# RWKV time mixing: mixing every unit on VectorE instead of projecting two of them unmixed, and a reordered tail

## The chip, the cores and the metric

The kernel runs on one core of a Trainium2 chip. A core has five engines with a queue each: TensorE (matmuls), VectorE (elementwise, called DVE in the profile), ScalarE (ACT, activations and copies with a scale), GpSimd (POOL) and SyncE (SP, which only issues transfers here). The metric is the device time of one execution in microseconds (us), as the median over several runs.

## The reference

```python
x_prev = np.zeros_like(x)
x_prev[:, 1:, :] = x[:, :-1, :]
xv = x * time_mix_v + x_prev * (1 - time_mix_v)
xr = x * time_mix_r + x_prev * (1 - time_mix_r)
v = xv @ value_weight
r = xr @ receptance_weight
out = (1 / (1 + np.exp(-r)) * v) @ output_weight
```

x is 16 x 2048 x 256 in fp32 and every weight is 256 x 256. The key projection of the full reference does not reach the output. So each row needs two mixed inputs, two projections, a sigmoid, a product z and an output projection.

## The kernel before

The 16 x 2048 rows are cut into 64 units of 512 rows (a batch has 4). A unit passes through these steps:

- The rows arrive in SBUF (x_unit and x_bf). TensorE transposes them, eight 128 x 128 blocks (`transposes`, L189), so that the 256 features lie on partitions in two halves, ko = 0 and 1. ScalarE copies the result into xt (L199 for fp32, L206 for bf16). Rows are laid out so that four "slots" of 128 columns hold rows j, j+1, j+2, j+3 of each partition's run. The row before a row is then the same column of the slot before, and only one extra slot per unit has to be filled by small copies (`wrap_slots`, L393 and L394).
- The mix. The weights are multiplied by time_mix once, so the mixed input is x + c * x_prev with c = 1/time_mix - 1. VectorE makes the product c * x_prev (`scale`, L239) and then adds x (`add`, L263), for the receptance (m = 0) and the value (m = 1). From some unit on the product of ko = 1 is made by GpSimd (`scale_pool`, L250); near the end ScalarE makes some (`scale_act`, L471).
- TensorE projects the mixed input (`project`, L274: four matmuls of 512 columns) to r and to v, R and V below. ScalarE applies the sigmoid to r (L492). VectorE multiplies it with v, which gives z (L521).
- TensorE multiplies z with the output weight (`out_matmuls`, L298, called O below), ScalarE copies the result to SBUF (L331), and SP issues the store. O of a unit follows one unit later.

Units 0 and 1 differ. The receptance of unit 0 and the value of unit 1 are not mixed: `project_unmixed` (L288) multiplies x_prev with a second weight w_prev = (1 - time_mix) * w and x with w_bf, eight matmuls instead of four. VectorE prepares w_prev at L412 and L429, from tm_prev (L167).

The order of the work on each engine is the order in which the program issues it (`manual_schedule`); an instruction waits at the head of its queue until what it reads is ready. The main loop over g writes that order out. Dictionaries say in which pass what is made for later units: `products[g]` (products on VectorE), `sums[g]` (adds ahead of z of unit g), `held[g]` (adds behind it), `pooled[g]` (products for GpSimd). `advance(limit)` issues transposes up to a unit, T1, T2 and so on below. Each of the PSUM pools ps_v, ps_r and ps_o has one buffer, and ps_t has two.

At the end `last_unit` takes unit 63 in two halves of 256 columns. It projects r by halves, then for each half: value projection, z (L359), and one half of O of unit 62. Then follows O of unit 63: slots 0 and 1 together in ps_v, copied by VectorE, slot 2 copied by ScalarE, slot 3 copied by VectorE (copies at L315, stores at L308). Slot 2 is stored from the ScalarE queue, the others from SP.

At the start small matmuls on zeros (`warm_up`, L140) keep TensorE at work while the first transfers are under way: 21, then 2, and 15 after the first transposes.

Of the kernel before, what the change touches and what calls it, by code (L numbers as in the profile page):

```python
# [15 lines left out]
def kernel(  # L16
# [110 lines left out]
    w_prev = consts.tile([P, 2, KO, D], BF16)  # L127
# [26 lines left out]
    tm_prev = consts.tile([P, 2, KO], FP32)  # L154

    def coefficients():
        ps = ps_o_pool.tile([P, 2, KO], FP32, name="psum_o")
        nc.tensor.transpose(
            out=ps.rearrange("p m k -> p (m k)"), in_=tm_rows, identity=ident_f[: 2 * KO, : 2 * KO]
        )  # L160
        tm = consts.tile([P, 2, KO], FP32)
        nc.vector.tensor_copy(out=tm, in_=ps)
        nc.vector.tensor_scalar(
            out=tms, in0=tm, scalar1=0.0, scalar2=1e-30, op0=ALU.is_equal, op1=ALU.mult
        )
        nc.vector.tensor_tensor(out=tms, in0=tms, in1=tm, op=ALU.add)
        nc.vector.tensor_scalar(  # L167
            out=tm_prev, in0=tm, scalar1=-1.0, scalar2=1.0, op0=ALU.mult, op1=ALU.add
        )
        nc.vector.reciprocal(c_sb, tms)  # L170
        nc.vector.tensor_scalar(out=c_sb, in0=c_sb, scalar1=-1.0, scalar2=None, op0=ALU.add)
# [110 lines left out]
    def project_unmixed(ps, g, m, mo):  # L282

        c = g * (UJ + 1) * P
        parts = [(w_prev[:, m, ko], ko, c) for ko in range(KO)]
        parts += [(w_bf[:, m, ko], ko, c + P) for ko in range(KO)]
        for n, (w, ko, lo) in enumerate(parts):
            nc.tensor.matmul(  # L288
                out=ps[:, mo, :],
                lhsT=w[:, mo * P : (mo + 1) * P],  # L290
                rhs=xt[0][:, ko, lo : lo + TU],
                start=(n == 0),
                stop=(n == len(parts) - 1),
            )

# [47 lines left out]
    def last_unit(g):  # L343
# [13 lines left out]
        for h, (lo, hi) in enumerate(cols):  # L357
            project(banks[2 + h], g, 1, lo, hi)
            nc.vector.tensor_tensor(  # L359
                out=z_sb[:, :, lo:hi], in0=s_sb[:, :, lo:hi], in1=banks[2 + h], op=ALU.mult  # L360
            )
# [46 lines left out]

    first_transposes()
    tile_for(0)  # L410
    for ko in range(KO):
        nc.vector.tensor_scalar(  # L412
            out=w_prev[:, 0, ko, :],
            in0=w_f32[:, 0, ko, :],
            scalar1=tm_prev[:, 0, ko : ko + 1],
            scalar2=None,
            op0=ALU.mult,
        )
    nc.vector.tensor_scalar(
        out=w_bf[:, 0, 0, :], in0=w_f32[:, 0, 0, :], scalar1=tms[:, 0, 0:1], scalar2=None, op0=ALU.mult  # L420
    )
    nc.scalar.activation(
        out=w_bf[:, 0, 1, :], in_=w_f32[:, 0, 1, :], func=ACT.Copy, scale=tms[:, 0, 1:2]
    )
    scale(pieces(0)[1])
    add(pieces(0)[1])
    for w, scale_by in [(w_bf, tms), (w_prev, tm_prev)]:
        for ko in range(KO):
            nc.vector.tensor_scalar(  # L429
                out=w[:, 1, ko, :],  # L430
                in0=w_f32[:, 1, ko, :],
                scalar1=scale_by[:, 1, ko : ko + 1],
                scalar2=None,
                op0=ALU.mult,
            )
# [11 lines left out]
    for u in range(2, NU):  # L447
# [31 lines left out]
    for g in range(NU - 1):  # L479
        ps_r = ps_r_pool.tile([P, KO, TU], FP32, name="psum_r")  # L480
        if g == 0:
            project_unmixed(ps_r, 0, 0, 0)
            advance(1)
            project_unmixed(ps_r, 0, 0, 1)
            for ko in range(KO):
                wrap_slots(pieces(1)[0], ko)
                scale(pieces(1)[0], (ko,))
            last = add(pieces(1)[0])
        else:
            project(ps_r, g, 0)  # L490
        s_sb = zpool.tile([P, KO, TU], BF16, name="s_sb")
        nc.scalar.activation(out=s_sb, in_=ps_r, func=ACT.Sigmoid)  # L492
        advance(START_T[g] if g < len(START_T) else g + LOOK)
        for p in products.get(g + 1, []):
# [15 lines left out]
        pool, name = (ps_o_pool, "psum_o") if g == 1 else (ps_v_pool, "psum_v")  # L510
        ps_v = pool.tile([P, KO, TU], FP32, name=name)
# [50 lines left out]
```

## Time and profile before

| | |
|---|---|
| median of 4 runs | 213.64 us (213.39 to 214.43) |
| profiled execution, its time | 213.33 us |
| its span (first to last instruction event) | 211.6 us |
| TensorE busy | 202.4 us, 96% |
| VectorE busy | 193.0 us, 91% |
| ScalarE busy | 185.8 us, 88% |
| GpSimd busy | 76.5 us, 36% |
| granted TensorE clock, mean | 0.994 |

In the rows of a timeline the first number is the start in us from the beginning of the span and the second the time that the group takes. Then come the engine, the line of the kernel, the operation, what it writes and reads, the sizes, and how many instructions were merged (x4). In brackets stands how long the engine had been idle before and what ended that. PEld is TensorE's loading of weights, which overlaps with matmuls. Consecutive instructions of an engine overlap a little in the records, so the distance between two starts is shorter than the duration shown. In the chain of work that ended last each row is a start, a time and the engine and line that held the chain then.

### The profile page before, as it was taken

To read this page: it belongs to the slowest core of one execution; us is meant where nothing else is said; L and a number is where in the kernel's file an instruction comes from. 1 tells how busy PE (TensorE), PEld (TensorE's weight loads), DVE (VectorE), ACT (ScalarE), POOL (GpSimd) and SP (SyncE) were. 2 spreads that over 40 slices of the span, in tenths; PEclk is the share of its full clock that TensorE was granted. 3 is DMA by queue.
4 is the path that set the end of the run, shared out by engine and by line. 5 is a ranking of instruction groups with operands and counts; after the bars stand their busy time and mean duration, and the time that the engine had idled before them with its cause. 6 is when DMAs were issued, how large, how long until landed. Compare 5 with 4: busy or idle time off the path is not lost.

```text
span 211.6 us, 4191 instructions
## 1 busy us (share of the span) xinstructions
PE 202.4 (96%) x1565; PEld 135.1 (64%) x1593; DVE 193.0 (91%) x321; ACT 185.8 (88%) x203; POOL 76.5 (36%) x106
## 2 busy tenths in 40 slices
PE   8789999999999999999999999999999999999991
PEld 7456665666666666666666666666666666665570
DVE  2789999999999999999999999999999999999971
ACT  3559999998999999999999999999999999999881
POOL 2701231334354435434452444335344432444200
PEclk9999999999999999999999999999999999999997
DMA  5999999999989998999989999897999944433475
GB/s 163 300 213 221 239 249 259 297 205 360 218 217 263 296 228 325 197 345 181 285 243 232 336 192 349 156 318 208 274 299 206 367 204 198 198 149 152 198 299 200
DMA packets 10140, 52.04 MB, mean 246 GB/s; under 512 B 1028, under 2 KB 2056, under 8 KB 5000
## 3 DMA queue, kind: packets, MB, share of 16 engines
q0 software_dynamic: 3008, 16.12, 44.1%
q1 hardware_dynamic: 6960, 35.52, 41.5%
q8 instruction: 12, 0.20, 0.3%
q10 hardware_dynamic: 152, 0.13, 0.2%
q14 instruction: 8, 0.07, 0.1%
HBM read 34.34 MB, written 33.55 MB: 321 GB/s over the span
## 4 chain that ended last, share of the span: by engine, by line
PE 74%; DVE 11%; DMA 5%; issue 4%; ACT 3%; POOL 1%; DVEq 0%; SPq 0%; POOLq 0%
PE psum_o L298 22%; PE psum_v L274 20%; PE psum_r L274 20%; PE ps_t L189 10%; DMA x_unit<-in_x_dram 5%; DVE mix L263 4%; DVE z_sb L521 3%; DVE mix L239 3%; ACT s_sb L492 2%; ACT xt_first L206 1%; PE psum_o L288 1%; ACT o_sb L331 0%; PE ps_t L274 0%; POOL mix L250 0%; DVE o_sb L315 0%
## 5 line engine op out<-in xcount | busy, mean ns | idle before, releaser
L250 POOL TENSOR_SCALAR mix<-xt,c_sb 128x1024 bf16<-128x1024 bf16 (+1 forms) x55 | 60.3, 1096 | 101.9 <-DVE mix L263 94.6
L263 DVE TENSOR_TENSOR mix<-mix,xt 128x1024 bf16<-128x1024 bf16 x112 | 78.1, 699 | 2.9 <-DVE mix L239 0.5
L521 DVE TENSOR_TENSOR z_sb<-s_sb,psum_v 128x1024 bf16<-128x1024 bf16 x62 | 75.5, 1217 | 4.6 <-PE psum_v L274 2.0
L331 ACT COPY o_sb<-psum_o 128x1024 f32<-128x1024 f32 x60 | 61.0, 1017 | 11.9 <-PE psum_o L298 11.9
L274 PEld LDWEIGHTS <-w_bf 128*128 128x128 bf16 x512 | 47.6, 98 | 33.7 <-issue 1.5
L492 ACT ACTIVATE s_sb<-psum_r 128x1024 bf16<-128x1024 f32 x63 | 65.1, 1033 | 0.5 <-PE psum_r L288 0.2
L274 PE MATMUL psum_v<-mix,w_bf 128*128 128x512 bf16 (+1 forms) x242 | 63.2, 377 | 0.8 <-DVE z_sb L521 0.2
L298 PE MATMUL psum_o<-wo_bf,z_sb 128*128 128x256 bf16 x488 | 63.4, 273 | 0.2
L274 PE MATMUL psum_r<-mix,w_bf 128*128 128x512 bf16 (+1 forms) x235 | 62.4, 377 | 0.6
L298 PEld LDWEIGHTS <-z_sb 128*128 128x128 bf16 x512 | 50.0, 98 | 19.0 <-DVE z_sb L359 0.3
L206 ACT COPY xt<-ps_t 128x1024 bf16<-128x1024 bf16 x56 | 57.0, 1022 | 0.0
L189 PEld LDWEIGHTS <-x_bf 128*128 128x128 bf16 x488 | 32.1, 98 | 13.5
L189 PE MATMUL ps_t<-ident,x_bf 128*128 128x128 bf16 x488 | 36.7, 219 | 0.3
L239 DVE TENSOR_SCALAR mix<-xt,c_sb 128x1024 bf16<-128x1024 bf16 (+1 forms) x63 | 27.7, 451 | 0.0
L263 DVE TENSOR_TENSOR mix<-mix,xt_first 128x1024 bf16<-128x1024 bf16 x14 | 9.5, 685 | 0.1
L106 POOL DMA_DIRECT2D x_bf<-in_x_dram x14 | 8.1, 576 | 0.0
L239 DVE TENSOR_SCALAR mix<-xt_first,c_sb 128x512 bf16<-128x512 bf16 x24 | 7.1, 348 | 0.3
L250 POOL TENSOR_SCALAR mix<-xt_first,c_sb 128x512 bf16<-128x512 bf16 x4 | 2.8, 692 | 12.6 <-DVE xt_first L394 12.6
L206 ACT COPY xt_first<-ps_t 128x1024 bf16<-128x1024 bf16 x5 | 5.2, 1037 | 1.1 <-PE ps_t L189 1.1
L140 PE MATMUL ps_t<-zeros 128*128 128x128 bf16 x38 | 3.8, 275 | 1.0 <-DVE zeros L84 1.0
L199 ACT CAST xt_first<-ps_t 128x512 bf16<-128x512 f32 x4 | 2.1, 589 | 2.7 <-PE ps_t L189 2.7
L140 PEld LDWEIGHTS <-zeros 128*128 128x128 bf16 x38 | 3.2, 125 | 1.0 <-DVE zeros L84 1.0
(67 smaller groups left out, 48.9 us busy)
## 6 DMA issues: line engine op xcount, KB each, us to landing
out_dram<-o_sb SPq DMA_DIRECT2D x30, 1024.0 KB, 8.3
x_bf<-in_x_dram POOLq DMA_DIRECT2D x14, 1024.0 KB, 11.4
x_bf<-in_x_dram POOLq DMA_DIRECT2D x5, 256.0 KB, 8.2
out_dram<-o_sb SPq DMA_DIRECT2D x5, 256.0 KB, 2.7
x_unit<-in_x_dram SPq DMA_DIRECT2D x2, 512.0 KB, 6.3
x_unit<-in_x_dram SPq DMA_DIRECT2D x2, 256.0 KB, 2.9
out_dram<-o_sb SPq DMA_DIRECT2D x1, 512.0 KB, 2.7
w_f<-n_receptance_weight_dram SPq DMA_DIRECT2D x1, 256.0 KB, 4.9
```

The costliest lines, as they stand in the source:

```text
L106: nc.gpsimd.dma_start(out=x_bf[b], in_=rows(b))
L140: nc.tensor.matmul(out=ps, lhsT=zeros, rhs=zeros, start=True, stop=True)
L189: nc.tensor.transpose(out=ps[:, jj * P : (jj + 1) * P], in_=src[:, jj, ko * P : (ko + 1) * P], identity=idn,)
L206: nc.scalar.copy(out=xt[b][:, :, c0 : c0 + TU], in_=ps)
L239: nc.vector.tensor_scalar(out=mix[b][:, m, ko, lo:hi], in0=xt[b][:, ko, c : c + hi - lo], scalar1=c_sb[:, m, ko : ko + 1], scalar2=None, o ...
L250: op = nc.gpsimd.tensor_scalar(out=mix[b][:, m, 1, lo:hi], in0=xt[b][:, 1, c : c + hi - lo], scalar1=c_sb[:, m, 1:2], scalar2=1.0, op0=ALU ...
L263: return nc.vector.tensor_tensor(out=mix[b][:, m, :, lo:hi], in0=mix[b][:, m, :, lo:hi], in1=xt[b][:, :, c : c + hi - lo], op=ALU.add,)
L274: nc.tensor.matmul(out=ps[:, mo, :], lhsT=w_bf[:, m, ko, mo * P : (mo + 1) * P], rhs=mix[b][:, m, ko, e * TU + lo : e * TU + hi], start=(k ...
L298: nc.tensor.matmul(out=ps[:, slot, :], lhsT=z[:, ko, jj * P : (jj + 1) * P], rhs=wo_bf[:, ko, :], start=(ko == 0), stop=(ko == KO - 1),)
L331: nc.scalar.copy(out=o_sb[b][:, j0 : j0 + UJ, :], in_=ps)
L492: nc.scalar.activation(out=s_sb, in_=ps_r, func=ACT.Sigmoid)
L521: nc.vector.tensor_tensor(out=z_sb, in0=s_sb, in1=ps_v, op=ALU.mult)
```

## The change

- `project_unmixed`, w_prev and tm_prev are removed. Unit 0's receptance is mixed as all others, in two pieces: slot 3 first, then slots 0 to 2. Both receptance weights are now made by VectorE (before, one of them by ScalarE). Of the value weights one is made by VectorE and one by ScalarE.
- In pass 0 the transposes T1 are issued ahead of R0. Behind R0 the loop now makes both mixes of unit 1, ahead of z of unit 0. Of unit 1's value mix the product of ko = 0 is made by ScalarE, issued ahead of unit 0's sigmoid.
- In pass 1 V1 and T3 are issued ahead of the mixes (these are on other engines), and unit 2's two mixes are made one after the other, product, add, product, add, both ahead of z of unit 1. The value add of unit 2 was behind that z before.
- The rule by which GpSimd makes the ko = 1 product of a value mix holds from unit 3 on (w > 1) instead of unit 4, and unit 3's slot copy is now made ahead of z of unit 1.
- In `last_unit` each half of O of unit 62 is issued ahead of the value projection of that half instead of behind it. O of unit 63 is taken in four single slots: slot 0 in ps_v copied by ScalarE, slot 1 in ps_o copied by VectorE, and slots 2 and 3 as before.

```diff
@@ last_unit
-        for h, (lo, hi) in enumerate(cols):
+        def value(h):
+            lo, hi = cols[h]
             project(banks[2 + h], g, 1, lo, hi)
             nc.vector.tensor_tensor(
                 out=z_sb[:, :, lo:hi], in0=s_sb[:, :, lo:hi], in1=banks[2 + h], op=ALU.mult
             )
+
+        def before(h):
             pool, name = [(ps_o_pool, "psum_o"), (ps_r_pool, "psum_r")][h]
             out_part(pool, name, z_prev, b, e - 1, h * H, H, by_act, nc.sync)
-        out_part(ps_v_pool, "psum_v", z_sb, b, e, 0, H, by_dve, nc.sync)
-        out_part(ps_t_pool, "ps_t", z_sb, b, e, H, 1, by_act, nc.scalar)
-        out_part(ps_t_pool, "ps_t", z_sb, b, e, H + 1, 1, by_dve, nc.sync)
+
+        before(0)
+        value(0)
+        before(1)
+        value(1)
+        out_part(ps_v_pool, "psum_v", z_sb, b, e, 0, 1, by_act, nc.sync)
+        out_part(ps_o_pool, "psum_o", z_sb, b, e, 1, 1, by_dve, nc.sync)
+        out_part(ps_t_pool, "ps_t", z_sb, b, e, 2, 1, by_act, nc.scalar)
+        out_part(ps_t_pool, "ps_t", z_sb, b, e, 3, 1, by_dve, nc.sync)
@@ head
+    def weight(m, ko, by_act=False):
+        ...
     first_transposes()
     tile_for(0)
     for ko in range(KO):
-        nc.vector.tensor_scalar(out=w_prev[:, 0, ko, :], ...)
-    nc.vector.tensor_scalar(out=w_bf[:, 0, 0, :], ...)
-    nc.scalar.activation(out=w_bf[:, 0, 1, :], ...)
+        weight(0, ko)
+    for lo, hi in [(UJ - 1, UJ), (0, UJ - 1)]:
+        part = (0, 0, lo * P, hi * P)
+        scale(part)
+        add(part)
     scale(pieces(0)[1])
     add(pieces(0)[1])
-    for w, scale_by in [(w_bf, tms), (w_prev, tm_prev)]:
-        ...
+    weight(1, 0)
     warm_up(WARM2)
@@ plan
-        (held if u - 1 < AHEAD else sums)[u - 1].append(p1)
+        (held if 2 <= u - 1 < AHEAD else sums)[u - 1].append(p1)
...
-            if paired or m == 1 and w > 2 and u != PAIRS - 1:
+            if paired or m == 1 and w > 1 and u != PAIRS - 1:
@@ main loop
     for g in range(NU - 1):
+        if g == 0:
+            advance(1)
+            weight(1, 1, by_act=True)
         ps_r = ps_r_pool.tile([P, KO, TU], FP32, name="psum_r")
+        project(ps_r, g, 0)
         if g == 0:
-            project_unmixed(ps_r, 0, 0, 0)
-            advance(1)
-            project_unmixed(ps_r, 0, 0, 1)
+            p0, p1 = pieces(1)
             for ko in range(KO):
-                wrap_slots(pieces(1)[0], ko)
-                scale(pieces(1)[0], (ko,))
-            last = add(pieces(1)[0])
-        else:
-            project(ps_r, g, 0)
+                wrap_slots(p0, ko)
+                scale(p0, (ko,))
+            add(p0)
+            scale_act(p1, (0,))
+            scale(p1, (1,))
+            last = add(p1)
         s_sb = zpool.tile([P, KO, TU], BF16, name="s_sb")
         nc.scalar.activation(out=s_sb, in_=ps_r, func=ACT.Sigmoid)
...
+        if g == 1:
+            ps_v = values()
...
+        left = list(sums[g])
         for p, kos in products[g]:
             if not (g - 1 + LOOK >= NU and p[1] == 1):
                 scale(p, kos)
-        for p in sums[g]:
+            if g == 1:
+                last = add(p)
+                left.remove(p)
+        for p in left:
             last = add(p)
...
-        if g == 1:
-            for mo in range(KO):
-                project_unmixed(ps_v, 1, 1, mo)
-            advance(3)
-        else:
-            project(ps_v, g, 1)
-        if g == 0:
-            advance(2)
+        if g != 1:
+            ps_v = values()
```

`values()` takes the PSUM buffer of V, issues `project(ps_v, g, 1)` and, for g < 2, `advance(g + 2)`.

More of the change, by code (lines that the diff above doesn't have):

```diff
@@ L126 @@
     w_bf = consts.tile([P, 2, KO, D], BF16)
-    w_prev = consts.tile([P, 2, KO, D], BF16)
     wo_bf = consts.tile([P, KO, D], BF16)
@@ L153 @@
     c_sb = consts.tile([P, 2, KO], FP32)
-    tm_prev = consts.tile([P, 2, KO], FP32)
     def coefficients():
@@ L166, in coefficients @@
         nc.vector.tensor_tensor(out=tms, in0=tms, in1=tm, op=ALU.add)
-        nc.vector.tensor_scalar(
-            out=tm_prev, in0=tm, scalar1=-1.0, scalar2=1.0, op0=ALU.mult, op1=ALU.add
-        )
         nc.vector.reciprocal(c_sb, tms)
@@ L280, in project @@
                 )
[L282 to L294, printed above, removed]
     def out_matmuls(ps, z, jj, slot):
@@ L407, in advance @@
             tnext += 1
+    def weight(m, ko, by_act=False):
+        scale_by = tms[:, m, ko : ko + 1]
+        if by_act:
+            nc.scalar.activation(
+                out=w_bf[:, m, ko, :], in_=w_f32[:, m, ko, :], func=ACT.Copy, scale=scale_by
+            )
+        else:
+            nc.vector.tensor_scalar(
+                out=w_bf[:, m, ko, :],
+                in0=w_f32[:, m, ko, :],
+                scalar1=scale_by,
+                scalar2=None,
+                op0=ALU.mult,
+            )
     first_transposes()
@@ L411 @@
     for ko in range(KO):
[L412 to L424, printed above, removed]
+        weight(0, ko)
[3 more added lines that the diff above has]
+        add(part)
     scale(pieces(0)[1])
     add(pieces(0)[1])
-    for w, scale_by in [(w_bf, tms), (w_prev, tm_prev)]:
[L428 to L435, printed above, removed]
+    weight(1, 0)
     warm_up(WARM2)
@@ L493, with values @@
         advance(START_T[g] if g < len(START_T) else g + LOOK)
+        def values():
+            pool, name = (ps_o_pool, "psum_o") if g == 1 else (ps_v_pool, "psum_v")
+            ps_v = pool.tile([P, KO, TU], FP32, name=name)
+            project(ps_v, g, 1)
+            if g < 2:
+                advance(g + 2)
+            return ps_v
+        if g == 1:
+            ps_v = values()
         for p in products.get(g + 1, []):
@@ L509 @@
             wrap_slots(p)
-        pool, name = (ps_o_pool, "psum_o") if g == 1 else (ps_v_pool, "psum_v")
-        ps_v = pool.tile([P, KO, TU], FP32, name=name)
-        if g == 1:
-            for mo in range(KO):
-                project_unmixed(ps_v, 1, 1, mo)
-            advance(3)
-        else:
-            project(ps_v, g, 1)
-        if g == 0:
-            advance(2)
+        if g != 1:
+            ps_v = values()
         z_sb = zpool.tile([P, KO, TU], BF16, name="z_sb")
```

## The prediction

> **What bounds the kernel now.** I read the busy row first. TensorE is busy 96% of the span, VectorE 91%, ScalarE 88%, so two or three engines are close to being the bound and an average does not decide. I therefore looked at the chain of work that ended last, in order of time, to see where it changes engine.
>
> ```profile
> 45.05 0.60 DVE mix L239 x3
> 46.04 0.47 issue
> 46.50 1.21 DVE z_sb L521
> 47.76 1.02 PE psum_v L274 x4
> 48.78 0.88 PE psum_o L298 x8
> 49.66 0.65 PE psum_r L274 x3
> ```
>
> Up to 46.50 the chain runs through VectorE (earlier pieces of the view, from 19.46 on, are the same lines L263, L239, L521 and L394). From 47.76 on it runs through TensorE. In the timeline value projections then start every 3.04 us (50.80, 53.85, 56.90), TensorE without a gap. The first 46 us are a VectorE chain of back-to-back work, and whatever moves that chain moves the rest of the kernel by the same amount. Over the stretch 19.5 to 46.5 VectorE is busy 27.00 of 27.00 us, TensorE 26.50.
>
> So the question is when VectorE can start the product z of unit 2, from where its cycle is unbroken. Its timeline at the head:
>
> ```profile
> 6.59 0.62 DVE L412 TENSOR_SCALAR w_prev<-w_f,tm_prev 128x256 bf16<-128x256 f32 x2 [1.64 <-DMA w_f<-n_receptance_weight_dram]
> 7.38 0.61 DVE L239 TENSOR_SCALAR mix<-xt_first,c_sb 128x512 bf16<-128x512 bf16 x2
> 8.02 0.69 DVE L263 TENSOR_TENSOR mix<-mix,xt_first 128x1024 bf16<-128x1024 bf16 x1
> ...
> 11.53 1.21 DVE L521 TENSOR_TENSOR z_sb<-s_sb,psum_v 128x1024 bf16<-128x1024 bf16 x1
> 13.29 0.23 DVE L394 COPY xt_first<-xt_first 128x254 bf16<-128x254 bf16 x1 [0.55 <-ACT xt_first L199]
> 13.63 1.14 DVE L239 TENSOR_SCALAR mix<-xt_first,c_sb 128x512 bf16<-128x512 bf16 x4
> 14.69 0.68 DVE L263 TENSOR_TENSOR mix<-mix,xt_first 128x1024 bf16<-128x1024 bf16 x1
> 15.29 1.22 DVE L521 TENSOR_TENSOR z_sb<-s_sb,psum_o 128x1024 bf16<-128x1024 bf16 x1
> ...
> 17.35 1.14 DVE L239 TENSOR_SCALAR mix<-xt_first,c_sb 128x512 bf16<-128x512 bf16 x4
> 19.46 1.22 DVE L521 TENSOR_TENSOR z_sb<-s_sb,psum_v 128x1024 bf16<-128x1024 bf16 x1 [0.23 <-ACT s_sb L492]
> ```
>
> Two things are to be seen. VectorE has only two waits after 6.59: 0.55 us before 13.29 (for the transposes of unit 2, whose transfer lands at 11.39) and 0.23 us before 19.46. Those are all the cover that added work can use. And starts are closer than durations: products of 512 columns follow each other every 0.26 us (0.35 long), adds every 0.60 (0.69 long), z every 1.13 (1.22 long). A product whose result the next add reads at once costs more, 0.64 us for two (7.38 to 8.02) where four independent ones cost 1.06 (13.63 to 14.69). I count starts.
>
> **TensorE, what is removed.** The unmixed projections take 8 matmuls where a mixed one takes 4, so 8 go: 4 in unit 0, 4 in unit 1, at 0.215 us each (8 from 13.29 to 15.01), 1.72 us together. Unit 0's four are not on any path: before, the first four of its eight ran while TensorE would have waited anyway.
>
> ```profile
> 7.00 0.39 PE L288 MATMUL psum_r<-xt_first,w_prev 128*128 128x512 bf16 x1 [0.95 <-DVE w_prev L412]
> 7.98 1.09 PE L189 MATMUL ps_t<-ident_f,x_unit 128*128 128x128 f32 x8
> ```
>
> The transposes T1 that follow wait for the transfer of x_unit, so putting them ahead of R0 leaves them at 7.98 (to 8.92). R0 then starts at about 9.0 and ends at 9.87, where it ended at 9.77. Unit 1's four matmuls do bring T3, the first output projection and ScalarE's chain forward by 0.86 us. That is worth only what VectorE, which is later, lets through.
>
> **VectorE, summed from 6.59.** Two receptance weights, 0.53: 7.12. Unit 0's receptance mix in two pieces (128 and 384 columns, each two products and an add) is not in the trace. Products of 512 and 1024 columns last 0.35 and 0.48 us (the L239 rows), which makes 0.25 for 128 and 0.31 for 384; for the add I take twice that slope, from 0.69 at 1024 elements: 0.29 and 0.56. With the starts 0.09 earlier than the ends, and 0.06 each time that an add waits for its product, the six come to 1.74 us. From below the whole unit in one piece bounds it, 1.25 (7.38 to 8.63); from above two pieces that each pay the 0.64 of a full pair, 2.1. The interpolation stays nearest to rows, so I take 1.74: 8.86. [...]
>
> Unit 0's value mix, 0.64 + 0.61: 10.11. One value weight, 0.27 (the other goes to ScalarE): 10.38. Unit 1's receptance mix with its slot copies, as before 1.84 (9.69 to 11.53): 12.22. Unit 1's value mix is new here, one product 0.39 and an add 0.61: 13.22. Then z of unit 0, which started at 11.53; it ends at 14.35. The 0.55 us wait is gone by then, as unit 2's copies are ready at 13.3. Slot copy of unit 2, 0.33 (13.29 to 13.63): 14.68. Its two mixes come one after the other, each 0.64 + 0.60, where four products together cost 1.06: 17.16. Slot copy of unit 3 ahead of z, 0.13: 17.29. z of unit 1: 18.42. Unit 3 has three products left on VectorE, 0.79, an add 0.60, a slot copy 0.13: 19.94. There z of unit 2 starts, against 19.46: **0.48 us later**. Cross-check as net work: removed 1.06 (w_prev), 0.27 (a value weight), 0.27 (a product of unit 3), 0.20 (its slot copy no longer ahead of a reader); added 0.27, 1.74, 1.00, 0.22; net 1.43. The two waits, counted in starts as all else, cover 0.64 and 0.31. That leaves 0.48.
>
> **What hides the rest.** The product on ScalarE is ahead of the sigmoid of unit 0 in its queue and waits for VectorE's slot copy at 10.64. By the ScalarE rows (0.51 for 256 columns, 1.15 for 1024) it takes about 0.7, so the sigmoid slides from 9.97 to about 11.3 and ends at 12.3, and behind it are T2's copies, 12.2 to 13.3, as before. z of unit 0 at 13.22 covers this by 0.9 us; without cover it would cost the 1.3 in full. The value weight on ScalarE is ready at 10.2, V0 runs 10.5 to 11.4 and T2 waits until 11.5 for its transfer regardless. The product of unit 3 on GpSimd (0.69) starts near 17.3 under z of unit 1, and is wanted only at 21. No input transfer is moved.
>
> From 19.94 the VectorE cycle is unchanged to z of unit 10, so V11 starts at 48.24, and TensorE's fixed pace carries +0.48 to the end.
>
> **The tail.**
>
> ```profile
> 204.04 0.60 PE L274 MATMUL psum_v<-mix,w_bf 128*128 128x256 bf16 x4
> 204.47 0.60 PE L298 MATMUL psum_o<-wo_bf,z_sb 128*128 128x256 bf16 x4
> 204.91 0.60 PE L274 MATMUL ps_t<-mix,w_bf 128*128 128x256 bf16 x4
> 205.62 0.69 DVE L359 TENSOR_TENSOR z_sb<-s_sb,ps_t 128x512 bf16<-128x512 bf16 x1 [0.18 <-PE ps_t L274]
> 206.36 0.33 PEld L298 LDWEIGHTS <-z_sb 128*128 128x128 bf16 x4 [0.26 <-DVE z_sb L359]
> 207.03 0.41 DVE L315 COPY o_sb<-ps_t 128x256 f32<-128x256 f32 x1
> ```
>
> With the previous unit's output parts (O62) moved ahead of the value projections, the second value half ends 0.44 us later (four matmuls of 256 columns), and TensorE is idle before 206.36 for that half's z. So the last two slots move by +0.43: last matmul 207.23, VectorE's copy 207.45 to 207.86 instead of 207.03 to 207.44. The single slots take the 0.69 us copy away from in front of it (0.41 instead, at 206.7), but it no longer waits there. The SP queue issued the last three stores at 206.60, 207.40 and 207.84, the last 0.40 after its copy; now it issues O62's second half at 206.3 and the slots at about 206.8, 207.5 and 208.2, one issue (0.33) more, none of it queued. That is +0.36 at the last issue. Landing took 2.7 us behind 256 KB issued 0.44 us earlier; with 128 KB ahead of it I expect 0.1 us less, and the shortest landing in the trace is 2.0. Bounds: 0 and +0.45; I take **+0.25**.
>
> **Sum.** 0.48 + 0.25 = +0.73 us on the profiled execution: span 211.6 to 212.3, its time 213.33 (1.73 around the span) to 214.06. The median of the runs, 213.64, is 0.31 above that execution, so 214.4. That is +0.34%, inside the 0.5% (1.07 us) that a measurement of this kernel can tell from no change.
>
> **Rivals.** *TensorE's saving comes through* (0.10). For it speaks the 0.86 us by which unit 1 is shorter; against it that TensorE's idle time between 12.4 and 47.8 is only about 0.9 us and is caused by VectorE. It takes the pieces at 1.25 (0.49 less) and dependent adds that do not wait (0.22 less) to bring the head to -0.23, 213.4 with no loss in the tail; the whole 0.86 gives 212.8, and for it VectorE must need 1.34 us less than summed. *It moves nothing* (0.11): pieces at 1.25 us use up no more than the two waits, and the lighter store queue takes the tail back: 213.6 to 213.8. *Slower, by the clock* (0.09): TensorE is idle from 6.04 (end of the second warm-up) to 7.98, 1.94 us, where it was idle 0.95. The trace has half speed at the start: warm-up matmuls every 0.11 us at 0.99, fp32 transposes 0.21 apart at 3.73, 0.116 from 4.15 on, so some 3.2 us of work to get out of it. If the wait at 6.04 to 7.98 falls back to it, T1, R0, V0 and T2 take 3.5 us more between them, of which waits at 8.9, 9.9 and 11.4 absorb about half, VectorE's slot copy of unit 2 comes at 15.4 instead of 14.35, and the sum is +1.05 more: 215.4. It decides from the point where T2's copies end after 14.35. [...]
>
> **How the numbers follow.** Main case 0.70, 213.6 to 215.1: 0.48 with -0.5 to +0.5 for pieces and waits on dependent adds, and the tail's bounds. About 0.16 of it lies above 214.71. With the clock case slower has 0.25. Faster than 212.57 needs the first rival nearly whole: 0.04. Within: 0.71. The range leaves out most of the clock case and the lower half of the first rival: 213.1 to 215.3.
>
> **What would show it.** R0 as 4 matmuls ending near 9.9 after T1 at 7.98; z of unit 0 near 13.2, of unit 1 near 17.3, of unit 2 near 19.9, without a wait on VectorE between 6.6 and 20; the change of engine in the chain at z of unit 10, near 47.0; V at 3.04 us afterwards; the last VectorE copy ending 5.1 us after z of unit 62 starts, where it is 4.67 now (202.77 to 207.44). Wrong if z of unit 2 starts before 19.4, if T1's transposes are 0.2 us apart, or if the last two slots wait for the stores.

## The result

The changed kernel takes 213.81 us (median of 36 runs, 213.25 to 214.62), the kernel before 213.59 us in the runs beside it (55 runs). The ratio is 1.001 with a 95% interval from 0.9998 to 1.0022: no difference that can be measured, with +0.22 us between the medians. A few executions of the kernel before took over 1.5% longer than its fastest; ratios and spreads leave them out. Forecast were 214.4 us, +0.73, in a range from 213.1 to 215.3, and no measurable change as the likeliest case.

In the tables and views below, the same work has other line numbers in the changed kernel: products L234, adds L258, slot copies L384, z L520, R and V L269, T1 and T2 L184, O L279, the copies at the end L296 and their stores L289.

The chain of work that ended last still changes from VectorE to TensorE at z of unit 10, 0.28 us later than before:

```profile
46.32 0.46 issue
46.78 1.22 DVE z_sb L520
48.00 0.04 issue
48.04 1.02 PE psum_v L269 x4
49.07 0.87 PE psum_o L279 x8
```

VectorE's timeline of the changed kernel, from the receptance weights to z of unit 2:

```profile
5.05 0.62 DVE L406 TENSOR_SCALAR w_bf<-w_f,tms 128x256 bf16<-128x256 f32 x2
5.59 0.46 DVE L234 TENSOR_SCALAR mix<-xt_first,c_sb 128x128 bf16<-128x128 bf16 x2
6.08 0.29 DVE L258 TENSOR_TENSOR mix<-mix,xt_first 128x256 bf16<-128x256 bf16 x1
6.29 0.56 DVE L234 TENSOR_SCALAR mix<-xt_first,c_sb 128x384 bf16<-128x384 bf16 x2
6.88 0.56 DVE L258 TENSOR_TENSOR mix<-mix,xt_first 128x768 bf16<-128x768 bf16 x1
...
9.26 0.35 DVE L406 TENSOR_SCALAR w_bf<-w_f,tms 128x256 bf16<-128x256 f32 x1 [0.55 <-DMA w_f<-in_value_weight_dram]
...
9.97 0.20 DVE L384 COPY xt_first<-xt_first 128x127 bf16<-128x127 bf16 x1 [0.28 <-ACT xt_first L194]
...
12.82 1.21 DVE L520 TENSOR_TENSOR z_sb<-s_sb,psum_v 128x1024 bf16<-128x1024 bf16 x1
13.95 0.22 DVE L384 COPY xt_first<-xt_first 128x254 bf16<-128x254 bf16 x1
...
16.93 1.22 DVE L520 TENSOR_TENSOR z_sb<-s_sb,psum_o 128x1024 bf16<-128x1024 bf16 x1
...
19.59 1.22 DVE L520 TENSOR_TENSOR z_sb<-s_sb,psum_v 128x1024 bf16<-128x1024 bf16 x1
```

The reader sees the six instructions of unit 0's receptance mix (5.59 to 7.36, so 1.77 us; 1.74 were summed), z of unit 0 followed without a wait by everything up to z of unit 2, and z of unit 2 at 19.59, 0.13 later than before. It also shows what the sum did not have: the receptance weights were used at 5.05 and not at 6.59, VectorE then waited 0.55 us for the value weights and 0.28 us for T1's copies. Nothing in the change moves these transfers. T1 started late too:

```profile
5.06 1.00 PE L139 MATMUL ps_t<-zeros 128*128 128x128 bf16 x15
8.69 1.06 PE L184 MATMUL ps_t<-ident_f,x_unit 128*128 128x128 f32 x8 [2.62 <-DMA x_unit<-in_x_dram]
```

TensorE's idle time is 2.62 us, not the 1.94 of the sum, and the eight transposes after it still take 1.06 us, at a granted clock of 1.00.

In the tail, the rows that answer to those of before, and the last copy:

```profile
204.32 0.60 PE L279 MATMUL psum_o<-wo_bf,z_sb 128*128 128x256 bf16 x4
204.76 0.60 PE L269 MATMUL psum_v<-mix,w_bf 128*128 128x256 bf16 x4
206.34 0.69 DVE L341 TENSOR_TENSOR z_sb<-s_sb,ps_t 128x512 bf16<-128x512 bf16 x1 [0.19 <-PE ps_t L269]
207.09 0.61 PE L279 MATMUL ps_t<-wo_bf,z_sb 128*128 128x256 bf16 x4 [0.26 <-DVE z_sb L341]
207.74 0.42 DVE L296 COPY o_sb<-ps_t 128x256 f32<-128x256 f32 x1 [0.37 <-PE ps_t L279]
```

The last copy ends at 208.16 instead of 207.44, 0.72 later, but the execution is only 0.52 longer (213.85 against 213.33). The end of the kernel does not follow the last copy. Of the difference 0.28 is there at V11, 0.08 more at the issue of the last store (208.20 against 207.84), and the rest comes behind it.

### The profile page after: what moved, and what is told of

It is laid out like the page before. It is cut to its first block, busy times and chain, and to the rows that moved or that the text cites. A ratio compares the mean times of both kernels' runs of the same rounds, so it can differ in the third digit from the quotient of the medians.

```text
span 212.0 us, 4187 instructions
## 1 busy us (share of the span) xinstructions
PE 201.3 (95%) x1558; PEld 134.1 (63%) x1585; DVE 194.5 (92%) x323; ACT 186.6 (88%) x205; POOL 77.1 (36%) x107
## 4 chain that ended last, share of the span: by engine, by line
PE 72%; DVE 13%; issue 6%; ACT 3%; DMA 3%; SPq 1%; POOL 0%; DVEq 0%; POOLq 0%
PE psum_o L279 22%; PE psum_v L269 20%; PE psum_r L269 19%; PE ps_t L184 10%; DVE mix L258 5%; DVE mix L234 4%; DVE z_sb L520 3%; DMA x_unit<-in_x_dram 3%; ACT s_sb L484 2%; ACT xt_first L194 1%; DVE xt_first L384 1%; PE ps_t L279 1%; PE ps_t L269 0%; SPq L116 0%; DVE z_sb L341 0%
## 5 line engine op out<-in xcount | busy, mean ns | idle before, releaser
L258 DVE TENSOR_TENSOR mix<-mix,xt 128x1024 bf16<-128x1024 bf16 x112 | 78.4, 702 | 2.5
L520 DVE TENSOR_TENSOR z_sb<-s_sb,psum_v 128x1024 bf16<-128x1024 bf16 x62 | 75.5, 1218 | 4.4 <-PE psum_v L269 2.3
L269 PEld LDWEIGHTS <-w_bf 128*128 128x128 bf16 x520 | 48.2, 98 | 35.8 <-issue 1.6
L269 PE MATMUL psum_r<-mix,w_bf 128*128 128x512 bf16 (+1 forms) x243 | 63.8, 377 | 0.8 <-DVE mix L258 0.3
L269 PE MATMUL psum_v<-mix,w_bf 128*128 128x512 bf16 (+1 forms) x238 | 63.0, 377 | 1.3 <-DVE mix L258 0.4
L279 PE MATMUL psum_o<-wo_bf,z_sb 128*128 128x256 bf16 x490 | 63.8, 273 | 0.2
L279 PEld LDWEIGHTS <-z_sb 128*128 128x128 bf16 x512 | 49.8, 98 | 19.7 <-DVE z_sb L341 0.8
L184 PEld LDWEIGHTS <-x_bf 128*128 128x128 bf16 x488 | 32.1, 98 | 13.5
L184 PE MATMUL ps_t<-ident,x_bf 128*128 128x128 bf16 x488 | 36.7, 219 | 0.3
L234 DVE TENSOR_SCALAR mix<-xt,c_sb 128x1024 bf16<-128x1024 bf16 (+1 forms) x63 | 27.7, 451 | 0.0
L258 DVE TENSOR_TENSOR mix<-mix,xt_first 128x1024 bf16<-128x1024 bf16 (+2 forms) x17 | 11.1, 657 | 0.3
L234 DVE TENSOR_SCALAR mix<-xt_first,c_sb 128x512 bf16<-128x512 bf16 (+2 forms) x28 | 8.3, 348 | 0.2
L245 POOL TENSOR_SCALAR mix<-xt_first,c_sb 128x512 bf16<-128x512 bf16 x5 | 3.4, 687 | 11.6 <-DVE xt_first L384 11.6
L184 PE MATMUL ps_t<-ident_f,x_unit 128*128 128x128 f32 x16 | 2.1, 276 | 2.6 <-DMA x_unit<-in_x_dram 2.6
```

Of the source, the lines that this page charges most:

```text
L184: nc.tensor.transpose(out=ps[:, jj * P : (jj + 1) * P], in_=src[:, jj, ko * P : (ko + 1) * P], identity=idn,)
L234: nc.vector.tensor_scalar(out=mix[b][:, m, ko, lo:hi], in0=xt[b][:, ko, c : c + hi - lo], scalar1=c_sb[:, m, ko : ko + 1], scalar2=None, o ...
L245: op = nc.gpsimd.tensor_scalar(out=mix[b][:, m, 1, lo:hi], in0=xt[b][:, 1, c : c + hi - lo], scalar1=c_sb[:, m, 1:2], scalar2=1.0, op0=ALU ...
L258: return nc.vector.tensor_tensor(out=mix[b][:, m, :, lo:hi], in0=mix[b][:, m, :, lo:hi], in1=xt[b][:, :, c : c + hi - lo], op=ALU.add,)
L269: nc.tensor.matmul(out=ps[:, mo, :], lhsT=w_bf[:, m, ko, mo * P : (mo + 1) * P], rhs=mix[b][:, m, ko, e * TU + lo : e * TU + hi], start=(k ...
L279: nc.tensor.matmul(out=ps[:, slot, :], lhsT=z[:, ko, jj * P : (jj + 1) * P], rhs=wo_bf[:, ko, :], start=(ko == 0), stop=(ko == KO - 1),)
```

## The experiments

All were timed against the kernel before on the same chip. Ratios are to that kernel, with 95% intervals; "changed" is the changed kernel above.

| run | median us | before beside it | ratio |
|---|---|---|---|
| new tail alone | 213.08 | 213.65 | 0.9971 (0.9949 to 0.9994) |
| new head alone | 213.81 | 213.65 | 1.0009 (0.9993 to 1.0026) |
| changed, one add less | 213.64 | 213.65 | 1.0000 (0.9981 to 1.0018) |
| changed, four matmuls less | 214.07 | 213.65 | 1.0029 (1.0010 to 1.0048) |
| changed, no second warm-up | 213.92 | 213.45 | 1.0031 (1.0012 to 1.0051) |
| single slots alone | 213.55 | 213.45 | 1.0003 (0.9988 to 1.0018) |
| changed, unit 0 unmixed | 212.89 | 213.45 | 0.9980 (0.9967 to 0.9993) |
| the same, O62 in its old place | 213.25 | 213.45 | 0.9997 (0.9979 to 1.0015) |
| O62's order alone | 212.93 | 213.51 | 0.9965 (0.9945 to 0.9985) |
| new tail alone, again | 213.39 | 213.51 | 0.9992 (0.9971 to 1.0013) |
| unit 0 unmixed, a product on GpSimd | 213.11 | 213.51 | 0.9989 (0.9962 to 1.0016) |
| unit 0 unmixed, O62's order alone | 212.79 | 213.61 | 0.9965 (0.9949 to 0.9981) |

### Head and tail apart

The new tail on the kernel before; the edit is that part of the diff:

```diff
+        before(0)
+        value(0)
+        before(1)
+        value(1)
+        out_part(ps_v_pool, "psum_v", z_sb, b, e, 0, 1, by_act, nc.sync)
+        out_part(ps_o_pool, "psum_o", z_sb, b, e, 1, 1, by_dve, nc.sync)
```

> The kernel before with the new tail alone (each half of O62 ahead of its value projection, O63 in four single slots). If the tail costs what I summed, the time is 0.25 us above the kernel before (0 to +0.45), and the last VectorE copy ends 5.1 us after z of unit 62 starts instead of 4.67. If single slots pay instead (a lighter store queue at the end), it is equal or up to 0.2 us below. The head is that of before, so z of unit 2 stays near 19.5.

Measured: 0.57 below, ratio 0.9971. In its trace the last copy ends 5.13 us after z of unit 62 starts (202.62 to 207.75), as summed, and yet the stretch from V11 to the end of the span is about 163.6 us, where the kernel before has 163.8. The mechanism on the engines was right, its consequence for the end was not.

The changed kernel with the old tail:

```diff
-        before(0)
-        value(0)
-        before(1)
-        value(1)
+        for h, (lo, hi) in enumerate(cols):
+            project(banks[2 + h], g, 1, lo, hi)
+            ...
+            out_part(pool, name, z_prev, b, e - 1, h * H, H, by_act, nc.sync)
```

> The changed kernel with the old tail. If VectorE sets the head as I summed it, from the receptance weights at 6.6 on, z of unit 2 starts near 19.9 and the time is 0.48 us above the kernel before. If the order in which transfers land sets it, as the profile after suggests (weights used at 5.05, T1 at 8.7), z of unit 2 is at 19.6 and the time is 0.1 to 0.3 above. If TensorE's saving of 0.86 us comes through, it is 0.4 to 0.9 below.

Measured: +0.16 by the medians, ratio 1.0009. TensorE's saving does not come through, and the full 0.48 does not appear either. The interval (0.9993 to 1.0026) includes both nothing and +0.5, so the time alone does not settle the size. In its trace z of unit 2 starts at 19.25, sooner than in the kernel before.

### Which engine holds the first 48 us

One VectorE add left out (the value mix of unit 5 then lacks its x):

```diff
         for p in held[g]:
-            add(p)
+            if g != 4:
+                add(p)
```

> The changed kernel without one VectorE add: the value mix of unit 5 lacks its x (left out of the computation). If VectorE is the bound until z of unit 10, everything after it comes 0.60 us earlier than in the changed kernel, so about 0.4 below the kernel before, and V11 starts near 47.4 instead of 48.04. If TensorE is the bound there, the time stays that of the changed kernel, about 0.2 above before.

Four matmuls left out (R and V of unit 4 use one half of the features):

```diff
-        project(ps_r, g, 0)
+        project(ps_r, g, 0, kos=1 if g == 4 else KO)
-            project(ps_v, g, 1)
+            project(ps_v, g, 1, kos=1 if g == 4 else KO)
```

> The changed kernel without four matmuls in pass 4: R4 and V4 use only one half of the features (the other half is left out of the computation). If VectorE is the bound there, nothing moves: V11 near 48.0, the time about 0.2 above the kernel before, as the changed kernel. If TensorE is the bound, the time is 0.86 below the changed kernel, about 0.65 below before.

The start of the head differs between executions, so the traces are compared from z of unit 2 to V11. That is 28.45 us in the changed kernel (19.59 to 48.04), 28.46 without the four matmuls (20.34 to 48.80), and 28.08 without the add (20.48 to 48.56). TensorE is not the bound there: 0.86 us of its work taken away moves nothing, and the median, 214.07, is not below the changed kernel either. VectorE is, but other engines are close behind: of 0.60 us 0.37 came through. (By the medians this run equals the kernel before, where 0.4 below was expected; the clock fell in 4 of its 22 executions, as shown below, and the median of the others is 213.37, 0.28 below.) The slot copy ahead of z of unit 5 starts at 29.68, and z would follow 0.13 behind it; it starts at 30.04, just behind the ends of its sigmoid on ScalarE (29.91) and of V of unit 5 on TensorE (29.94):

```profile
28.84 1.07 ACT L484 ACTIVATE s_sb<-psum_r 128x1024 bf16<-128x1024 f32 x1
28.91 1.03 PE L269 MATMUL psum_v<-mix,w_bf 128*128 128x512 bf16 x4
...
29.68 0.23 DVE L384 COPY xt_first<-xt_first 128x254 bf16<-128x254 bf16 x1
...
30.04 1.22 DVE L520 TENSOR_TENSOR z_sb<-s_sb,psum_v 128x1024 bf16<-128x1024 bf16 x1
```

Both engines work without a gap here, so the next limit is ScalarE or TensorE, about 0.4 us behind VectorE; this trace does not tell which.

### What sets z of unit 2

Times from the profiled execution of each kernel, in us: first use of the receptance weights (w), start of T1 and of T2, start of z of unit 2, and its distance to the one that sets it.

| kernel | w | T1 | T2 | z of unit 2 | distance |
|---|---|---|---|---|---|
| before | 6.59 | 7.98 | 11.52 | 19.46 | T2 + 7.94 |
| new tail alone | 6.49 | 8.36 | 11.38 | 19.32 | T2 + 7.94 |
| new tail alone, again | 5.28 | 7.40 | 11.06 | 19.00 | T2 + 7.94 |
| single slots alone | 5.74 | 7.89 | 12.13 | 20.07 | T2 + 7.94 |
| O62's order alone | 6.18 | 9.12 | 11.78 | 19.86 | T2 + 8.08 |
| changed | 5.05 | 8.69 | 11.54 | 19.59 | T1 + 10.90 |
| new head alone | 5.74 | 7.76 | 10.62 | 19.25 | w + 13.51 |
| changed, four matmuls less | 6.80 | 8.22 | 12.40 | 20.34 | w + 13.54 |
| changed, no second warm-up | 5.99 | 7.47 | 11.78 | 19.43 | w + 13.44 |

With the old head, z of unit 2 follows T2, thus the third x transfer, at a fixed distance in four of five rows. In the fifth, O62's order alone, the value weights landed late and VectorE works without a wait from 9.75, when it first uses them. With the new head it follows VectorE's work, from the receptance weights (13.5 us, where the sum had 13.35) or, when x's second transfer is late, from T1. T2 is covered in every row of the new head (in the run without four matmuls its copies end at 14.14 and VectorE is busy with z of unit 0 until 14.71; that z of unit 2 is 7.94 behind T2 there too is chance). The transfers themselves land at other times in each execution: w varies by 1.75 us and T2 by 1.8 over these rows. An estimate from the five rows with the old head, with the later of w + 13.5 and T1 + 10.9 put in place of what is there, moves z of unit 2 by +0.63, +0.67, -0.22, -0.83 and +0.16, on average by +0.1: which head is sooner depends on the landings. The spread of the timed runs fits only in part. The standard deviation is 0.33 to 0.43 us in the four kernels with the new head and second warm-up, without the executions in which the clock fell, and 0.54 to 0.66 in the groups of the kernel before; but other kernels with the old head have 0.44 to 0.84.

### The mix of unit 0 undone

```diff
-    for ko in range(KO):
-        weight(0, ko)
-    for lo, hi in [(UJ - 1, UJ), (0, UJ - 1)]:
-        part = (0, 0, lo * P, hi * P)
-        scale(part)
-        add(part)
+    # two w_prev weights on VectorE, as before
+    ...
+        if g == 0:
+            project_unmixed(ps_r, 0)
+            advance(1)
+            weight(1, 1, by_act=True)
+            project_unmixed(ps_r, 1)
```

> The changed kernel with unit 0's receptance unmixed again (eight matmuls for R0, two w_prev weights, no mix of unit 0's receptance on VectorE). If VectorE's work between the receptance weights and z of unit 0 is what the changed head costs, z of unit 2 starts 7.2 us after T2 starts (near 18.7 when T2 is at 11.5) instead of 7.94 as in the kernel before, and with the new tail the time is 0.7 to 1.3 us below the kernel before. If the mix of unit 0 is not what costs, the time is that of the changed kernel, 0.2 above before.

Measured: 0.56 below by the medians, ratio 0.9980, less than the 0.7 to 1.3 expected. The named distance was wrong: z of unit 2 came 8.04 after T2, and T2 did not set it: it follows T1 at 10.93 (9.15 to 20.08). T1's chain, with unit 1's two mixes ahead of z of unit 0 on it, is as long with the mix of unit 0 (10.90) as without. What the undoing removes is the other start, the 13.5 us from the receptance weights: in the four traces with unit 0 unmixed z of unit 2 follows T1 each time.

The same with O62 in its old place and single slots:

> As the run before this one (unit 0's receptance unmixed again), with O62 in its old place and O63 in four single slots. If both steps add up, 0.1 to 0.4 us below that run; if O62's new order was worth something, above it.

Measured: ratio 0.9997, 0.36 us above the run before it by the medians. So the order of O62 was worth something, the case that I had named last. In the trace z of unit 2 is at T1 + 10.92 again.

One product less on VectorE (GpSimd makes the ko = 1 product of unit 1's value mix):

```diff
-            scale(p1, (1,))
+            nc.gpsimd.tensor_scalar(
+                out=mix[0][:, 1, 1, TU : 2 * TU], ..., scalar1=c_sb[:, 1, 1:2], scalar2=1.0,
+                op0=ALU.mult, op1=ALU.mult,
+            )
```

> The kernel with unit 0's receptance unmixed again and the new tail, with one more product off VectorE: GpSimd makes the ko = 1 product of unit 1's value mix. In the trace of the kernel without this step z of unit 2 started 10.93 us after T1. If VectorE's work from T1 on is the bound, z of unit 2 starts 10.6 after T1 (0.26 to 0.39 less), and the time is 0.8 to 1.0 us below the kernel before where 0.56 was measured. If the wait for GpSimd takes its place, nothing is gained.

Measured: z of unit 2 at T1 + 10.77 (8.25 to 19.02), a gain of 0.15 and not 0.3. The ratio, 0.9989, has both signs in its interval. Inconclusive for the time.

### The tail taken apart

Single slots alone, O62 in its old place:

```diff
-        out_part(ps_v_pool, "psum_v", z_sb, b, e, 0, H, by_dve, nc.sync)
+        out_part(ps_v_pool, "psum_v", z_sb, b, e, 0, 1, by_act, nc.sync)
+        out_part(ps_o_pool, "psum_o", z_sb, b, e, 1, 1, by_dve, nc.sync)
```

> The kernel before with O63 in four single slots, O62 left in its old place. In the run with the whole new tail the last VectorE copy ended 0.46 us later and the execution still 0.25 earlier after it. If the single slots make that gain (the store queue is lighter at the end), this one keeps the gain without the later copies: 0.4 to 0.9 us below the kernel before, and lower than the whole new tail. If the order of O62 makes it, the time is that of the kernel before.

Measured: ratio 1.0003. Single slots gain nothing that can be measured (0.9988 to 1.0018), which points to O62's order. That alone:

```diff
-            pool, name = [(ps_o_pool, "psum_o"), (ps_r_pool, "psum_r")][h]
-            out_part(pool, name, z_prev, b, e - 1, h * H, H, by_act, nc.sync)
+        before(0)
+        value(0)
+        before(1)
+        value(1)
```

> The kernel before with each half of O62 ahead of its value projection and O63 as before (slots 0 and 1 together). The last VectorE copy should end 0.4 us later. If the end of the execution is set by when the stores drain, and the sooner store of O62 is what the whole new tail gains, the time is 0.2 to 0.6 us below the kernel before. If the last copy sets it, 0.4 above; if order and single slots only gain together, the time is that of the kernel before.

Measured: 0.58 below, ratio 0.9965, with the last copy 0.45 later relative to z of unit 62 (203.16 to 208.28). And the whole new tail a second time:

> The kernel before with the whole new tail, a second time, beside the run with O62's order alone on the same chip. 0.57 us below the kernel before was measured, with an interval from 0.13 to 1.09. If the gain is real, 0.2 to 0.6 below; if the single slots cost what they cost with O62 in its old place (0.1), a little above the run with O62's order alone.

Measured: 0.12 below, ratio 0.9992; its interval includes no change at all. Over both runs of the whole tail the middle is about 0.35 below.

The store issues on the SP queue of the kernel before show why a later copy costs little:

```profile
205.72 0.33 SPq L308 DMA_DIRECT2D out_dram<-o_sb  x1
206.60 0.33 SPq L308 DMA_DIRECT2D out_dram<-o_sb  x1
207.40 0.33 SPq L308 DMA_DIRECT2D out_dram<-o_sb  x1
207.84 0.39 SPq L308 DMA_DIRECT2D out_dram<-o_sb  x1
```

The third store could go at 207.11, when slots 0 and 1 were copied, and went at 207.40, 0.80 after the one ahead of it. What makes it 0.80 is not shown. The last could go at 207.44 and went at 207.84. The queue was late, not the copy. With O62's order alone:

```profile
205.74 0.34 SPq L308 DMA_DIRECT2D out_dram<-o_sb  x1
206.57 0.33 SPq L308 DMA_DIRECT2D out_dram<-o_sb  x1
207.78 0.33 SPq L308 DMA_DIRECT2D out_dram<-o_sb  x1
208.31 0.56 SPq L308 DMA_DIRECT2D out_dram<-o_sb  x1
```

V of unit 62 starts 0.39 later in this execution (201.67 against 201.28). Counted from there, O62's two stores go 0.37 and 0.42 sooner, the last copy ends 0.45 later (6.61 against 6.16), and the last store goes 0.08 later (6.64 against 6.56), now 0.03 behind its copy. It also lands sooner: in the table of transfers the last 128 KB store takes 2.7 us in the kernel before and 2.4 here.

```profile
out_dram<-o_sb SPq DMA_DIRECT2D x5, 256.0 KB, 2.3
out_dram<-o_sb ACTq DMA_DIRECT2D x1, 128.0 KB, 2.5
out_dram<-o_sb SPq DMA_DIRECT2D x1, 128.0 KB, 2.4
```

0.08 - 0.3 makes about -0.2; from V of unit 62 to the end of the span it is about 10.0 us instead of 10.3. With single slots and O62 late, three stores wait behind each other: slots 0 and 1 are both copied at 207.47 and stored at 208.03 and 208.47, and the stretch is 10.5.

With the new head the tail's gain is not there. Head alone is at +0.16 and the changed kernel, with both parts, at +0.22. The last store and the landing of stores of its size, first with the new tail alone, then in the changed kernel:

```profile
207.78 0.53 SPq L308 DMA_DIRECT2D out_dram<-o_sb  x1
out_dram<-o_sb SPq DMA_DIRECT2D x3, 128.0 KB, 2.4
...
208.20 0.40 SPq L289 DMA_DIRECT2D out_dram<-o_sb  x1
out_dram<-o_sb SPq DMA_DIRECT2D x3, 128.0 KB, 2.9
```

The last store goes 160.16 us behind V11 in both (160.08 in the kernel before), but it lands later in the changed kernel: from its issue to the end of the span it is 3.8 us instead of 3.4. In all five traces with the mixed unit 0, the one with the old tail included, this is 3.8 to 4.0 us; in five of the six with O62 sooner and unit 0 unmixed it is 3.3 to 3.5, and in the sixth, with the product on GpSimd, 3.8. Why the landing differs stays open.

### The clock

One of the runs showed the rival that I had priced and put at 0.09. In the profiled execution with one add less, TensorE ends its warm-up at 6.51 and waits 2.32 us, until 8.84. Its transposes then take 1.94 us instead of 1.06, R0 1.72 instead of 1.03, and the stretches show the granted clock (the number ahead of the last two; the columns in front are busy times of PE, PEld, DVE, ACT and POOL):

```profile
6.00:8.00 2.00, 0.51 (x10) 0.34 (x7) 1.93 (x8) 0.32 (x1) 2.00 (x5) 1.00 1.06 376
8.00:10.00 2.00, 1.17 (x6) 1.20 (x7) 1.79 (x6) 0.04 (x1) 0.93 (x2) 0.64 1.10 231
10.00:12.00 2.00, 2.00 (x8) 1.09 (x7) 1.15 (x5) 1.73 (x4) 0.22 (x1) 0.51 1.20 213
12.00:14.00 2.00, 2.00 (x15) 1.39 (x13) 1.86 (x5) 1.73 (x3) 0.00 (x0) 1.00 1.13 211
```

In that execution VectorE waits 0.75 us for T1's copies, and z of unit 0 comes at 13.72. The two profiled executions with this fall have a mean granted clock of 0.986, the other twelve 0.993 or more. Counted by a mean below 0.99, there are 7 in the 102 timed runs of the four kernels with the changed head and second warm-up, 1 in the 220 of the kernel before, and none in the 160 of the other kernels with the old head or with unit 0 unmixed, where matmuls of R0 fall into the wait. In the run with most of them (4 of 22) their median is 214.75 against 213.37 for the others; the three other runs with one each have it 0.7 to 1.6 above their median of the others.

The length of the wait does not decide by itself. In this trace the granted clock is full up to 8.55, half from there to 11.97, thus for 3.41 us, and full again:

```profile
5.51 1.00 PE L139 MATMUL ps_t<-zeros 128*128 128x128 bf16 x15
8.84 1.94 PE L184 MATMUL ps_t<-ident_f,x_unit 128*128 128x128 f32 x8 [2.32 <-DVE mix L234]
...
8.50:8.55 0.05, 0.00 (x0) 0.00 (x0) 0.05 (x2) 0.00 (x0) 0.05 (x1) 1.00 0.92 225
8.55:8.60 0.05, 0.00 (x0) 0.00 (x0) 0.05 (x1) 0.00 (x0) 0.05 (x1) 0.55 0.49 102
...
11.90:11.95 0.05, 0.05 (x2) 0.05 (x1) 0.05 (x1) 0.05 (x1) 0.00 (x0) 0.50 1.37 256
11.95:12.00 0.05, 0.05 (x2) 0.05 (x1) 0.05 (x1) 0.05 (x1) 0.00 (x0) 0.82 0.94 174
12.00:12.10 0.10, 0.10 (x2) 0.00 (x0) 0.07 (x2) 0.10 (x1) 0.00 (x0) 1.00 1.30 241
```

In the run of the next experiment it is half from 8.05 to 11.46, again 3.41. In the 3.41 us ahead of each fall TensorE was at work for 1.37 us (5.14 to 6.51) and 1.38 us (4.63 to 5.43 and 7.47 to 8.05). Each of these stretches begins about where TensorE's fp32 transposes become faster: in the first trace they come 0.21 us apart up to 5.00, one takes 0.18, and from 5.18 on they come 0.11 apart; in the second trace three take 0.56 us from 4.16 and the fourth 0.11. In the changed kernel they become faster near 4.2 (two take 0.63 us at 3.73, four take 0.64 at 4.15); the stretches of 3.41 us counted from there hold about 1.9 and 2.3 us of work, as the longer wait of 2.62 us lies across both, and the clock did not fall. In these three traces the fall goes with the work in such a stretch and so with where the stretches lie, not with the length of the wait; no run tests this further.

The second warm-up taken out leaves less work ahead of T1:

```diff
-    warm_up(WARM2)
```

> The changed kernel without the second warm-up (15 small matmuls on zeros), so TensorE is idle from about 5.1 until T1, some 3 to 3.7 us instead of 2 to 2.6. If the fall to the slow clock comes with the length of that idle time, most executions fall (mean granted clock near 0.985) where 7 of 102 did in kernels with the changed head, and the median is 0.8 to 1.4 us above the changed kernel's 213.8. If those few executions had another cause, the share stays near 7% and the median near 213.8.

Measured: 7 of 22 fall, more often than 7%, less often than "most". In its trace the wait is only 2.04 us (5.43 to 7.47), because T1's transfer was early. The median is 0.47 above its kernel before where the changed kernel has 0.22, so the price is a fraction of what I expected, and the fallen executions do not take longer than the others here (213.75 against 214.08). Its trace shows a fall: T1 at 7.47 takes 1.41 us, R0 1.91, and z of unit 2 is at 19.43, because VectorE's work from the weights covers it. So less work ahead of T1 does raise the share (7 of 22 against 7 of 102). The fall did not lengthen these executions; that it costs time only where T1 is late as well fits both traces and is not shown further.

### The parts that gained, together

Unit 0 unmixed, unit 1 mixed, O62 sooner, slots 0 and 1 together:

> The parts that gained, together: unit 0's receptance unmixed, unit 1 mixed, O62 one place sooner, and O63 in slots 0 and 1 together. Against the kernel before 0.57 was measured with unit 0 unmixed and the whole new tail, and 0.58 with O62's order alone. If single slots cost 0.1 to 0.2, this one is 0.6 to 0.8 us below the kernel before. If head and tail do not add up because the landing of the first transfers sets the head in all of them, it is near 0.5 below.

Measured: 212.79, 0.82 below the kernel before by the medians, ratio 0.9965 (0.9949 to 0.9981). It is faster than the kernel before, and through that comparison than the changed kernel, which stood at 1.001; whether it beats O62's order alone, at the same ratio, these runs cannot tell.

## Why the prediction was right, and which steps were not

The forecast of no measurable change holds, and its middle was 0.5 us too high. In part this is luck. Head and tail were both summed too high, and the range was wide enough to hold the error; +0.22 is what the rival "it moves nothing" named (213.6 to 213.8), but not for its reasons, as the pieces took 1.77 us and not 1.25. By its own steps:

- **What bounds the kernel: right.** VectorE until z of unit 10, then TensorE at its pace, a value projection every 3.04 us. Taking matmuls away moved nothing (28.46 us from z of unit 2 to V11, against 28.45), taking an add away did (28.08). That ScalarE or TensorE is only about 0.4 us behind was not in the text.
- **The removed matmuls are worth nothing by themselves: right**, as far as four matmuls less in pass 4 moved nothing and the head alone came to +0.16.
- **VectorE's sum: right in its durations, wrong in its start.** From the receptance weights to z of unit 2, 13.35 us were summed and 13.44 to 13.54 came in the three traces where nothing else held it. The term that failed is the 0.48. It is the difference between a chain that starts at the weights and one that starts at the third x transfer, and I took both starts from one execution, in which the weights were late (6.59; six of the eight other traces of the table have 5.05 to 6.18). The 0.55 us wait that I counted as cover is not a property of the kernel: with O62's order alone VectorE does not have it. The head costs +0.1 by the estimate over five executions and +0.16 by the medians of the head alone, an amount that the runs do not tell from nothing.
- **Small instructions: the interpolation from rows was right.** Six instructions took 1.77 us, 1.74 were interpolated.
- **The tail: wrong in sign on the old head, and worth nothing on the new one.** The copies came 0.44 to 0.45 later behind V11, as summed. The step that failed is "+0.36 at the last issue": I kept the 0.40 us between the last copy and its store, which was the queue's delay behind the stores ahead of it. O62's stores go 0.4 sooner and clear the queue; the last store goes only 0.08 later. On the old head the tail gains about 0.2 to 0.3 in the traces, 0.35 by the medians of its two runs. On the new head the last store's landing takes it back, which the text had expected to be 0.1 us sooner.
- **The clock: its 0.09 was an estimate of mine, and the fall is real.** The longest wait of TensorE behind 4.15 in the trace of before is 0.95 us, so that a wait of 1.94 us would leave the clock as it was is not shown there. Here the fall came with waits of 2.32 and 2.04 us, and stayed away with 2.62 in the changed kernel's trace; the two stretches of 3.41 us that ended in a fall held 1.37 and 1.38 us of work. What decides which executions fall, 7 in 102, is not shown beyond these three traces. In price the rival was near: about 1.4 us in one run, 1.05 in the text.

Three steps are left that no view explains. With the changed head, z of unit 2 to V11 takes 28.45 us, with the old head and with unit 0 unmixed 28.28 to 28.30; the 0.16 us are lost at z of unit 3, which comes 3.42 us behind z of unit 2 instead of 3.26. V11 to V of unit 62 takes 153.68 instead of 153.52 in four of five traces with that head; this does not reach the last store, which goes 160.16 behind V11 with the new tail on either head. And the last stores land 0.4 to 0.5 us later than with the same tail on the old head, which takes back what the tail gains there; so the two parts do not add up. The causes stay open.

## What to carry to other kernels

Before counting a wait in one execution as cover, ask whether it ends with a transfer: early transfers landed up to 1.8 us apart between executions of the same code, and a sum over two chains with different starts has to use the spread, not one draw. At the end of a kernel look at the store queue and the time from issue to landing before counting copies: with the old head an earlier store of the previous unit was worth more than an earlier last copy. Time two parts of a change together as well as apart: this tail gained alone and gained nothing on the new head. The wait of TensorE ahead of its first dense work was a small risk to its clock here: 7 executions in 102 fell, and 1 in 380 of the kernels in which matmuls of R0 lie in that wait.

## What the runs showed of the hardware that I had not expected

- TensorE's granted clock fell from 1.00 to 0.50, for 3.41 us, behind a stretch of 3.41 us with 1.37 or 1.38 us of work, in two executions; with 1.9 us or more of work, and a longer wait, it did not in another.
- Stores on the SP queue whose copies are done follow each other at 0.44 to 0.48 us, and at 0.80 to 0.83 behind O62's second half, though most rows show 0.33 busy.
- The landing of the same first transfers differs between executions: first use of the receptance weights 5.05 to 6.80, start of T2, where it waited for its transfer, 11.06 to 12.40 us.
- The 128 KB stores of the SP queue at the end take 2.9 us to land (median of a trace) in every trace with the mixed unit 0, and 2.3 to 2.7 in all but one of the others.
